# A two-layer hybrid backbone: the norm chains of layer one's latent halves staggered in separate PSUM banks, and W1 in three column passes

## The chip, the cores and the metric

The kernel runs on one core of one Trainium2 chip, as one program. The metric is the device time of one execution in microseconds. The kernel before took 2814.94 us (median of three runs, 2808.75 to 2815.92).

## The reference

Two layers work on a stream of 512 latent tokens and 256 context tokens with 1024 channels. Each layer mixes tokens (an RWKV-7 scan and gated linear attention behind one input projection, a merge projection behind them) and then applies an MLP with squared ReLU. Each of the two parts is normed and modulated before and behind it. Cut to what matters here:

```python
m_lat, m_ctx, v_new = token_mixer(h_lat, h_ctx, v_first, lp, l, rows, not last)
x_lat = x_lat + g_m * rms_norm(m_lat, norm_mix_post[l])
f_lat = sq_relu_mlp(modulate(x_lat, norm_ffn_pre[l], sh_f, sc_f), mlp_w1[l], mlp_w2[l])
x_lat = x_lat + g_f * rms_norm(f_lat, norm_ffn_post[l])
if not last:
    x_ctx = x_ctx + cg_m * rms_norm(m_ctx, norm_mix_post[l])
    f_ctx = sq_relu_mlp(modulate(x_ctx, norm_ffn_pre[l], csh_f, csc_f), mlp_w1[l], mlp_w2[l])
    x_ctx = x_ctx + cg_f * rms_norm(f_ctx, norm_ffn_post[l])
```

`rms_norm` divides by the root of the mean square over a token's 1024 channels; `modulate` norms, scales and shifts. The context counts in layer one only; its output is not needed behind the last layer.

## The kernel before

Activations lie channel by channel: 8 tiles of 128 channels by 768 columns, of which 0 to 255 are the context ("c") and 256 to 767 the latents ("l"). For the norms the latents are cut in two halves of 256 columns, "l" and "l2". An fp32 product is made of three fp32r products: a weight tile of 128 x 1024 is loaded in two halves of 256 KB (`wr`, `load_w`), each split into `wh` by ACT and `wl` by POOL or DVE, and multiplied with the split activations `sh` and `sl`. So a weight tile is 24 matmuls for each pass over columns; the result stays in a PSUM bank `d`.

`out_mlp` is the part of a layer behind the mixer: the branches' output projection (`wout`), the merge projection (`wmrg`), then four blocks of W1 (8 tiles) and W2 (8 tiles). In layer one most tiles go over the 512 latent and the 256 context columns at once. Two places are woven instead: the merge with the beginning of W1's first block, and the last block of W2 with the first tiles (12, 13, 14) of the next layer's input projection (`first_tiles`). There the tiles go column pass by column pass, so that the norm chain of some columns can run beside the matmuls of others.

A norm chain is `post_mod`: the squares of the 8 tiles are summed (`sum_sq`: ACT writes `q` or `S`, POOL adds them, small matmuls with a column of ones sum over channels), DVE and POOL form the reciprocal root `rn`, two PE transposes spread it over the partitions into a PSUM bank, DVE multiplies (`u`) and DVE and POOL in turn add to the residual `x`. Then the same again on `x`, and ACT and DVE write the next `sh` and `sl`. Both the sum and the spread statistic of a chain use one bank tile from the pool that `CB` names for it: `D0` and `D1` are pools of one PSUM bank each. A bank's tiles are handed out in the order in which the code asks for them.

`weave` sets the order of the code: the steps are the tiles of the passes; each chain is a generator of five parts, and `at` says before which step each part is asked for (offsets -1, 1, 2, 5, 6 from the chain's own step). In layer one the first entry of `halves` holds two chains, l and l2, which are stepped together.

The code's order is not yet the order of execution. `Order` collects all instructions of a segment (`flush` ends one), gives each a price and a due time by its place in the code (dense matmuls are due later by a fixed amount), and places them engine by engine as inputs, banks and buffers come free by its prices. What it decides is then fixed for each engine's queue. PE, ACT, DVE, POOL and SP (the DMA queue) each work strictly in that order. Consecutive PE calls of one `kind` are placed as one node. A segment starts from the clocks at which the one before it ended.

Of the kernel before, what the change touches and what calls it, by code (L numbers as in the profile page):

```python
# [11 lines left out]
F32 = mybir.dt.float32  # L12
# [7 lines left out]
P = 128  # L20
D = 1024
KT = 8
NCTX = 256
NLAT = 512
NT = NCTX + NLAT
NCH = NT // 64
L0 = NCTX
# [71 lines left out]

SB = 6  # L100
ACCUM = (False, True)

CFG = {
    "nfill": ((2, 2, 0, 2, 2, 1, 1, 2, 0, 2, 2, 0, 2, 1, 1, 0, 0, 0, 0), (2, 3, 0, 2, 2, 1, 2, 2, 0, 2, 2, 0, 1, 0, 0, 1, 0, 0, 0)),
# [47 lines left out]
class Order:  # L152
# [57 lines left out]
    def add(self, key, op, fn, a, k):  # L210
        out = k["out"] if "out" in k else a[0]
        ins = [x for x in (*a[(0 if "out" in k else 1):], *(v for n, v in k.items() if n != "out")) if isinstance(x, bass.AP)]
        w, n = self.width, {}
# [5 lines left out]
        if key == "PE":  # L219
            lhs = k["lhsT"] if "lhsT" in k else a[1]  # L220
# [49 lines left out]
                else:  # L270
                    n["d"] = 150.0 + 1.05 * c + (60.0 if op == "scalar_tensor_tensor" and isinstance(k.get("scalar"), bass.AP) else 0.0)
        if key == "PE":
            n["kind"] = (n["cfg"], str(lhs.dtype), op, n["w"][0][0].cap_key if n["w"] else None)
            n["calls"] = 1
            n["fill"] = n["dense"] and bool(n["w"]) and str(n["w"][0][0].cap_key).startswith("d1")
            n["side"] = bool(n["w"]) and n["w"][0][0].name.startswith("da_")
            p = self.nodes[-1] if self.nodes else None
            if GROUP and p is not None and p.get("kind") == n["kind"] and p["calls"] < (3 if lhs.dtype == F32R else 8 if n["dense"] else 16):
                p["call"].append((fn, a, k))
                p["calls"] += 1  # L280
                p["d"] += n["d"]
                p["flow"] += n["flow"]
                for x in ("w", "r"):
                    p[x] += [y for y in n[x] if y not in p[x]]
                return
# [289 lines left out]
def hybrid_kernel(ctx: ExitStack, tc: tile.TileContext, A: dict, out: bass.AP):  # L575
# [74 lines left out]
    def mm(o, a, b, start=True, stop=True):  # L650
        pe.matmul(o, lhsT=a, rhs=b, start=start, stop=stop)
# [3 lines left out]
    class Ring:  # L655
        n = 0
# [13 lines left out]
            return dps.tile(shape, dt, name=name, tag=self.tag, bufs=1)  # L670

    D0, D1 = One("d0"), One("d1")
    CB = ({"l": D0, "l2": D0, "c": D1}, {"l": D0, "l2": D1})

    def load_w(src, slots=None, lo_eng=(pool, pool), qs=(0, 1), c=None):
        halves = []
# [205 lines left out]
    def weave(dd, dw, chains, offs, then=()):  # L882
        steps = [f for g in dd for f in g] + [f for g in dw for f in g]
        nt = len(dd[0])
        at = {}
        for gi, ch in enumerate(chains):
            lim = nt * len(dd) + len(dw[0]) * gi if dw else 999
            for off in offs:
                at.setdefault(min(nt * (gi + 1) + off, lim), []).append(ch)
        for p in range(max(len(steps), max(at) + 1)):  # L890
            for chs in at.get(p, ()):
                for ch in chs:
                    next(ch, None)
            if p < len(steps):
                steps[p]()
            for at_p, f in then:
                if p == at_p:
                    f()
# [12 lines left out]

    def first_tiles(l, acts, pss, s):
        tiles = [(pss[0], None, "", 12), (pss[1], mps, "d", 13), (pss[2], ips, "i", 14)]
        tiles = [t for t in tiles if l == 0 or s == "l" or t[3] != 14]
        n = NLAT if s == "l" else NCTX
        o = L0 if s == "l" else 0
        for q in range(2):
            for ps, pl, tag, m in tiles:
                if q == 0:
                    pl = pl or (D0 if s == "l" else D1)  # L920
                    ps[s] = pl.tile([P, 512], F32, name="d", tag=tag)[:, 0:n]
                (hi, lo), = load_w(A["win"][l, m], None, (dve, pool), (q,))
                for k in range(4):
                    ah, al = acts[k + 4 * q]
                    for wi, (wt, at) in enumerate(((hi, ah), (hi, al), (lo, ah))):
                        mm(ps[s], wt[:, k, :], at[:, o:o + n], start=(q == 0 and k == 0 and wi == 0),
                           stop=(q == 1 and k == 3 and wi == 2))

    def mixer(l, acts, adas, pre, early):
# [879 lines left out]
    def out_mlp(l, last, ya, wo):  # L1809
        full = l == 0  # L1810
        st = STREAMS if full else STREAMS[:1]
        groups = STREAMS if full else GROUPS[:2]
        halves = [GROUPS[:2], GROUPS[2:]] if full else [[g] for g in GROUPS[:2]]
        nf = 3 if full else 5
        o0 = 0 if full else L0
        n0 = NT - o0
        eng = lambda j: (pool, dve)[j % 2]
# [1 line left out]
        with ExitStack() as mx:  # L1819
# [21 lines left out]
                for m in ms_:  # L1841
                    evac(m, dense(load_w(srcs[m], None, PD), acts, st), st)

            def passes(srcs, acts, evac, ms_):
                def one(m, g):
                    evac(m, dense(load_w(srcs[m], None, PD), acts(), [g]), [g])

                return [[(lambda m=m, g=g: one(m, g)) for m in ms_] for g in groups]

            late, pre = {}, [{}, {}, {}]  # L1850

# [31 lines left out]
            for c in range(4):  # L1883
                hid = {}

                def ev_h(m, ps, sts):
                    if m not in hid:
                        hid[m] = alloc_hl(("bh", "bl"), bp)
                    o, n = min(x[1] for x in sts), sum(x[2] for x in sts)
                    t = tp.tile([P, n], F32, name="t", tag="t", bufs=3)  # L1890
                    for s, o1, n1 in sts:
                        act.activation(out=t[:, o1 - o:o1 - o + n1], in_=ps[s], func=AF.Relu)
                        dve.tensor_tensor(out=t[:, o1 - o:o1 - o + n1], in0=t[:, o1 - o:o1 - o + n1], in1=ps[s], op=ALU.mult)
                    hi, lo = hid[m]
                    act.activation(out=hi[:, o:o + n], in_=t, func=AF.Copy)
                    pool.tensor_tensor(out=lo[:, o:o + n], in0=t, in1=hi.bitcast(F32)[:, o:o + n], op=ALU.subtract)

                def ev_o(m, ps, sts):
                    for s, o, n in sts:
                        if c == 0:  # L1900
                            act.activation(out=ac[m][:, o:o + n], in_=ps[s], func=AF.Copy)
                        else:
                            dve.tensor_tensor(out=ac[m][:, o:o + n], in0=ac[m][:, o:o + n], in1=ps[s], op=ALU.add)

                w1 = [A["w1"][l, 8 * c + m] for m in range(8)]
                if c == 0:
                    weave(passes(wm, lambda: mh, ev_mrg, range(8)), passes(w1, new_h, ev_h, range(nf)),
                          [[post_mod(tp, ms, l, 1, g, xs, None, l, 2, new_h) for g in gs] for gs in halves], CFG["om"][l])
                    h = late.pop("h")
                    ac = [acc.tile([P, NT], F32, name="a", tag="a") for _ in range(8)]  # L1910
                body(w1, h, ev_h, range(nf if c == 0 else 0, 8))
                w2 = [A["w2"][l, c, m] for m in range(8)]
                hd = [hid[m] for m in range(8)]
                if c < 3:
                    body(w2, hd, ev_o, range(8))

            def store_x(j, x, o, n):
                if last:
                    sp.dma_start(out=out[:, j, o - L0:o - L0 + n], in_=x[:, o:o + n])
                else:  # L1920
                    sp.dma_start(out=xdr[0][:, j, o:o + n], in_=x[:, o:o + n])

            weave(passes(w2, lambda: hd, ev_o, range(8)), [],
                  [[post_mod(tp, ac, l, 3, g, xs, store_x, l + 1, 0, None if last else new_h) for g in gs] for gs in halves], CFG["oe"][l],
                  () if last else ((16, lambda: first_tiles(l + 1, late["h"], pre, "l")), (22, lambda: first_tiles(l + 1, late["h"], pre, "c"))))
            early = {} if last else {8: load_w(A["win"][l + 1, 8], c=0)}
            od.flush()
            return late.get("h"), pre, early
# [148 lines left out]
```

## Time and profile before

| | |
|---|---|
| three runs | 2808.75 to 2815.92 us, median 2814.94 |
| profiled execution | 2812.3 us, its span 2810.5 us |
| PE busy | 95% of the span |
| DVE, ACT, POOL busy | 58%, 46%, 42% |
| granted TensorE clock | 0.977 of full speed on average |
| DMA | 276.53 MB, mean 98 GB/s |

The page says what each engine did over the whole execution. Busy shares are averages over stages with different limits, so the stages have to be looked at one by one: the output part of layer one lies between about 860 and 1600 us of the span, the mixers on either side of it.

### The profile page before, as it was taken

Reading aid. Unit: us, or ns where it says so; the run is one execution under the profiler, and the core shown is the slowest. Engines: PE = TensorE matmul, PEld = TensorE weight load, DVE = VectorE, ACT = ScalarE, POOL = GpSimd, SP = SyncE. Lnnn points to the kernel's source line nnn. Section 1 sums busy time; section 2 is a strip of 40 time slices with the busy share of each in tenths; the row PEclk is TensorE's granted clock in tenths of the full one; section 3 lists DMA queues with packets and bytes.
Section 4 is the critical chain, followed back from the end, with each engine's and each line's share of the span. In section 5 each row is a group of like instructions: output and inputs, shape, how many; then the busy total and the mean of one; then the engine's idle time right before and its main releaser. Section 6 shows DMA issues by size and latency. Waiting matters only on the chain.

```text
span 2810.5 us, 56340 instructions
## 1 busy us (share of the span) xinstructions
PE 2662.9 (95%) x22618; PEld 2229.4 (79%) x22618; DVE 1624.6 (58%) x2996; ACT 1282.8 (46%) x2606; POOL 1179.3 (42%) x1336
## 2 busy tenths in 40 slices
PE   7999999999989999999999899999989979899998
PEld 5788878788767878888888777777777768888887
DVE  6687787886687361122223636887878687622224
ACT  5554545545553452322134545555555564533333
POOL 3653534433321642223135546554444232733335
PEclk9999999999999989999999899999999999999999
DMA  6321323232226322222223344321311126433334
GB/s 238 117 88 56 115 93 119 82 96 67 78 90 238 101 73 63 64 64 61 64 64 103 121 157 125 95 81 57 108 39 40 42 62 221 124 109 98 94 97 132
DMA packets 148437, 276.53 MB, mean 98 GB/s; under 512 B 16496, under 2 KB 25456, under 8 KB 148176
## 3 DMA queue, kind: packets, MB, share of 16 engines
q1 hardware_dynamic: 148176, 272.93, 30.7%
q8 instruction: 178, 2.92, 0.4%
q14 instruction: 83, 0.68, 0.1%
HBM read 242.85 MB, written 30.02 MB: 97 GB/s over the span
## 4 chain that ended last, share of the span: by engine, by line
PE 76%; DVE 9%; POOL 4%; ACT 4%; DMA 4%; issue 3%; SPq 0%; POOLq 0%; ACTq 0%; DVEq 0%
PE d L567 58%; PE c L567 8%; PE m L567 5%; PE i L567 4%; PE da L567 1%; POOL wl L567 1%; DVE lw L567 1%; DVE ZA L567 1%; POOL S L567 1%; POOL x L567 1%; DMA ra<-in_ada_dram 1%; DVE ZS L567 1%; ACT f L567 1%; DMA wr<-in_win_dram 1%; DVE sc L567 1%
## 5 line engine op out<-in xcount | busy, mean ns | idle before, releaser
L567 PE MATMUL d<-sh,wh 128*128 128x512 f32 (+1 forms) x3280 | 1192.0, 363 | 28.1 <-ACT f L567 10.8
L567 PE MATMUL d<-sh,wl 128*128 128x512 f32 (+1 forms) x3280 | 1138.3, 347 | 16.0 <-POOL wl L567 13.4
L567 PE MATMUL d<-sl,wh 128*128 128x512 f32 (+1 forms) x3280 | 1138.3, 347 | 3.0 <-POOL sl L567 1.7
L567 POOL TENSOR_TENSOR wl<-wr,wh 128x512 fp32r<-128x512 f32 x356 | 479.9, 1350 | 750.7 <-ACT wh L567 734.8
L567 PEld LDWEIGHTS d<-sh,wh 128*128 128x128 f32 x3280 | 629.2, 192 | 128.3 <-issue 18.1
L567 PEld LDWEIGHTS d<-sh,wl 128*128 128x128 f32 x3280 | 628.1, 191 | 99.8 <-POOL wl L567 18.7
L567 PEld LDWEIGHTS d<-sl,wh 128*128 128x128 f32 x3280 | 629.6, 192 | 69.8 <-DVE sl L567 3.8
L567 ACT ACTIVATE wh<-wr 128x512 fp32r<-128x512 f32 x580 | 362.1, 627 | 495.8 <-PE d L567 389.9
L567 DVE TENSOR_TENSOR wl<-wr,wh 128x512 fp32r<-128x512 f32 x224 | 170.9, 767 | 180.4 <-ACT wh L567 171.7
L567 DVE TENSOR_TENSOR t<-t,d 128x512 f32<-128x512 f32 (+1 forms) x101 | 58.1, 577 | 315.5 <-ACT t L567 315.5
L567 POOL TENSOR_TENSOR sl<-t,sh 128x512 fp32r<-128x512 f32 (+2 forms) x72 | 104.8, 1458 | 207.1 <-ACT sh L567 207.1
L567 DVE TENSOR_TENSOR a<-a,d 128x512 f32<-128x512 f32 (+1 forms) x80 | 44.4, 554 | 228.8 <-PE d L567 228.7
L567 ACT ACTIVATE XY<-i 128x512 f16<-128x512 f32 x192 | 108.2, 593 | 91.0 <-PE i L567 89.1
L567 ACT ACTIVATE t<-d 128x512 f32<-128x512 f32 (+1 forms) x101 | 51.4, 510 | 167.0 <-PE d L567 166.6
L567 POOL TENSOR_TENSOR LTL<-AB,LTB 64x512 f16<-64x512 f32 x48 | 61.0, 1271 | 136.3 <-DVE LTB L567 98.4
L567 POOL TENSOR_TENSOR rn<-rn,C 128x2 f32<-128x2 f32 (+2 forms) x41 | 60.2, 1468 | 119.2 <-DVE rn L567 118.5
L567 POOL TENSOR_TENSOR S<-S,q 128x256 f32<-128x256 f32 x92 | 75.7, 832 | 56.5 <-ACT q L567 53.7
L567 PEld LDWEIGHTS <-XY 64*64 64x64 f16 x1920 | 64.3, 109 | 40.5 <-issue 27.8
L567 DVE TENSOR_TENSOR Q<-i,MK 128x512 f16<-128x512 f32 x120 | 82.7, 689 | 18.3 <-PE i L567 15.5
L567 ACT ACTIVATE f<-d 128x512 f32<-128x512 f32 (+1 forms) x85 | 54.3, 647 | 82.4 <-PE d L567 65.5
L567 PE MATMUL i<-Q,XY 64*64 64x64 f16 x1920 | 80.5, 197 | 7.9 <-DVE Q L567 5.0
L567 PEld LDWEIGHTS <-LTB 128*128 128x128 f16 x1344 | 60.3, 99 | 26.9 <-issue 21.1
(258 smaller groups left out, 4193.2 us busy)
## 6 DMA issues: line engine op xcount, KB each, us to landing
wr<-in_w_dram SPq DMA_DIRECT2D x304, 256.0 KB, 2.7
wr<-in_win_dram SPq DMA_DIRECT2D x180, 256.0 KB, 2.9
wa<-in_ada_dram SPq DMA_DIRECT2D x160, 256.0 KB, 2.9
wr<-in_wmrg_dram SPq DMA_DIRECT2D x64, 256.0 KB, 3.0
ra<-in_ada_dram SPq DMA_DIRECT2D x32, 256.0 KB, 5.4
wr<-in_wout_dram SPq DMA_DIRECT2D x32, 256.0 KB, 3.2
gdr<-fg SPq DMA_DIRECT2D x20, 384.0 KB, 3.0
gdr<-fg SPq DMA_DIRECT2D x20, 256.0 KB, 2.0
```

Of the source, the lines that this page charges most:

```text
L567: ins = fn(*a, **k).ins
```

## The change

Five edits, all for layer one's output part:

- `CB`: the chain of l2 uses the bank pool D1 instead of D0; the context's chain stays on D1.
- `weave` and its callers: the three column groups l, l2 and c have a chain each instead of l and l2 being stepped together. With three chains, l's step is 8, l2's is 9 (`NB` = 1) and the context's 16.
- The first tiles of W1's first block: four (`NF`) instead of three, and over l, l2 and c with 256 columns each instead of over 512 latent and 256 context columns. Each pass loads its weight tiles anew. Four tiles instead of five are left for the plain form.
- `first_tiles`: l and l2 are separate calls, from step 15 (`F0`) and 17, which load their weights anew; before it was one call for 512 columns from step 16. Both write the same bank, l the columns 0 to 255 and l2 the others. The call for c stays at step 22.
- The planner's `kind` of a matmul also holds the tensor's name where both operands are the same tensor.

For layer two `parts` has the same two groups as `halves` had, and `nf` stays 5.

```diff
+NF = 4
+NB = 1
+F0 = 15
...
-            n["kind"] = (n["cfg"], str(lhs.dtype), op, n["w"][0][0].cap_key if n["w"] else None)
+            n["kind"] = (n["cfg"], str(lhs.dtype), op, n["w"][0][0].cap_key if n["w"] else None, lhs.tensor.name if lhs.tensor is rhs.tensor else None)
...
-    CB = ({"l": D0, "l2": D0, "c": D1}, {"l": D0, "l2": D1})
+    CB = ({"l": D0, "l2": D1, "c": D1}, {"l": D0, "l2": D1})
...
             lim = nt * len(dd) + len(dw[0]) * gi if dw else 999
+            t0 = (nt, nt + NB, 2 * nt)[gi] if len(chains) == 3 else nt * (gi + 1)
             for off in offs:
-                at.setdefault(min(nt * (gi + 1) + off, lim), []).append(ch)
+                at.setdefault(min(t0 + off, lim), []).append(ch)
...
-        tiles = [t for t in tiles if l == 0 or s == "l" or t[3] != 14]
-        n = NLAT if s == "l" else NCTX
-        o = L0 if s == "l" else 0
+        tiles = [t for t in tiles if l == 0 or s != "c" or t[3] != 14]
+        c0 = NCTX if s == "l2" else 0
+        o, n = {"l": (L0, NCTX), "l2": (L0 + NCTX, NCTX), "c": (0, NCTX)}[s]
         for q in range(2):
             for ps, pl, tag, m in tiles:
-                if q == 0:
+                sk = "c" if s == "c" else "l"
+                if q == 0 and s != "l2":
                     pl = pl or (D0 if s == "l" else D1)
-                    ps[s] = pl.tile([P, 512], F32, name="d", tag=tag)[:, 0:n]
+                    ps[sk] = pl.tile([P, 512], F32, name="d", tag=tag)[:, 0:NLAT if s == "l" else n]
...
-                        mm(ps[s], wt[:, k, :], at[:, o:o + n], start=(q == 0 and k == 0 and wi == 0),
+                        mm(ps[sk][:, c0:c0 + n], wt[:, k, :], at[:, o:o + n], start=(q == 0 and k == 0 and wi == 0),
...
-        halves = [GROUPS[:2], GROUPS[2:]] if full else [[g] for g in GROUPS[:2]]
-        nf = 3 if full else 5
+        parts = GROUPS if full else GROUPS[:2]
+        nf = NF if full else 5
...
-            def passes(srcs, acts, evac, ms_):
+            def passes(srcs, acts, evac, ms_, gs):
...
-                return [[(lambda m=m, g=g: one(m, g)) for m in ms_] for g in groups]
+                return [[(lambda m=m, g=g: one(m, g)) for m in ms_] for g in gs]
...
-                    weave(passes(wm, lambda: mh, ev_mrg, range(8)), passes(w1, new_h, ev_h, range(nf)),
-                          [[post_mod(tp, ms, l, 1, g, xs, None, l, 2, new_h) for g in gs] for gs in halves], CFG["om"][l])
+                    weave(passes(wm, lambda: mh, ev_mrg, range(8), groups), passes(w1, new_h, ev_h, range(nf), parts),
+                          [[post_mod(tp, ms, l, 1, g, xs, None, l, 2, new_h)] for g in parts], CFG["om"][l])
...
-            weave(passes(w2, lambda: hd, ev_o, range(8)), [],
-                  [[post_mod(tp, ac, l, 3, g, xs, store_x, l + 1, 0, None if last else new_h) for g in gs] for gs in halves], CFG["oe"][l],
-                  () if last else ((16, lambda: first_tiles(l + 1, late["h"], pre, "l")), (22, lambda: first_tiles(l + 1, late["h"], pre, "c"))))
+            weave(passes(w2, lambda: hd, ev_o, range(8), groups), [],
+                  [[post_mod(tp, ac, l, 3, g, xs, store_x, l + 1, 0, None if last else new_h)] for g in parts], CFG["oe"][l],
+                  () if last else ((F0, lambda: first_tiles(l + 1, late["h"], pre, "l")), (F0 + 2, lambda: first_tiles(l + 1, late["h"], pre, "l2")), (22, lambda: first_tiles(l + 1, late["h"], pre, "c"))))
```

## Rows read from the trace of the kernel before

**Rows 1.** The page: busy time, share of the span and instructions of each engine.

```profile
PE 2662.9 (95%) x22618; PEld 2229.4 (79%) x22618; DVE 1624.6 (58%) x2996; ACT 1282.8 (46%) x2606; POOL 1179.3 (42%) x1336
```

**Rows 2.** Table by stages: stretch, its length, busy us, PEclk, DMA share, GB/s.

```profile
942.00:1033.00 91.00, 78.97 (x438) 69.98 (x437) 55.54 (x109) 47.36 (x109) 57.31 (x61) 0.83 0.27 83
...
1075.00:1524.00 449.00, 449.00 (x2511) 391.63 (x2511) 88.53 (x146) 124.73 (x217) 125.00 (x90) 1.00 0.22 66
1524.00:1600.00 76.00, 64.04 (x368) 57.65 (x367) 54.68 (x111) 37.03 (x83) 47.70 (x51) 0.82 0.43 130
```

**Rows 3.** Timeline of PE, stage A: start, duration, instruction [idle before, who ended it].

```profile
948.86 0.28 PE L567 MATMUL d<-sh,wh 128*128 128x256 f32 x1
...
967.50 0.38 PE L567 MATMUL d<-sh,wl 128*128 128x256 f32 x1 [2.57 <-POOL wl L567]
...
993.74 0.66 PE L567 MATMUL d<-C,rn 128*128 128x128 f32 x2 [3.17 <-DVE u L567]
...
997.33 0.79 PE L567 MATMUL d<-sh,wh 128*128 128x512 f32 x1 [0.25 <-ACT sh L567]
...
1075.77 0.39 PE L567 MATMUL d<-sh,wh 128*128 128x512 f32 x1
```

**Rows 4.** Timeline of DVE: the second statistics in A, W2's last latent tile.

```profile
978.08 0.16 DVE L567 TENSOR_SCALAR rn<-d 128x2 f32<-128x2 f32 x1 [4.58 <-PE d L567]
...
984.69 0.16 DVE L567 TENSOR_SCALAR rn<-d 128x2 f32<-128x2 f32 x1 [2.86 <-PE d L567]
986.04 1.26 DVE L567 SCALAR_TENSOR_TENSOR u<-x,AB,d 128x256 f32<-128x256 f32 x3 [1.19 <-PE d L567]
...
1523.95 0.69 DVE L567 TENSOR_TENSOR a<-a,d 128x512 f32<-128x512 f32 x1 [4.29 <-PE d L567]
```

**Rows 5.** Timeline of PE, stage B.

```profile
1570.22 0.66 PE L567 MATMUL d<-C,rn 128*128 128x128 f32 x2 [5.73 <-DVE u L567]
...
1603.52 0.50 PE L567 MATMUL d<-sh,wh 128*128 128x512 f32 x1 [0.24 <-ACT f L567]
```

**Rows 6.** Timeline of PE in a quiet stretch: first matmuls of three runs of twelve.

```profile
1432.71 0.40 PE L567 MATMUL d<-sh,wh 128*128 128x512 f32 x1
...
1435.46 0.28 PE L567 MATMUL d<-sh,wh 128*128 128x256 f32 x1
...
1436.89 0.40 PE L567 MATMUL d<-sh,wh 128*128 128x512 f32 x1
```

**Rows 7.** Groups by shape, 950 to 1030, the chains' matmuls: busy us, mean ns | idle.

```profile
L567 PE MATMUL d<-C,S 128*128 128x1 f32 x68 | 11.4, 286 | 3.1 <-DVE u L567 2.0 <-POOL S L567 1.1
L567 PE MATMUL d<-C,rn 128*128 128x128 f32 x12 | 3.1, 354 | 3.4 <-DVE u L567 3.2
```

**Rows 8.** Groups by shape, POOL, 942 to 1033.

```profile
L567 POOL TENSOR_TENSOR wl<-wr,wh 128x512 fp32r<-128x512 f32 x15 | 20.2, 1344 | 8.1 <-ACT wh L567 8.1
L567 POOL TENSOR_TENSOR S<-S,q 128x256 f32<-128x256 f32 x24 | 18.5, 783 | 13.4 <-ACT q L567 13.1 <-POOL S L567 0.2
L567 POOL TENSOR_TENSOR x<-x,u 128x256 f32<-128x256 f32 x12 | 11.0, 923 | 2.2 <-DVE u L567 2.2
L567 POOL TENSOR_TENSOR rn<-rn,C 128x2 f32<-128x2 f32 x6 | 5.0, 842 | 5.0 <-DVE rn L567 5.0
...
L567 POOL TENSOR_TENSOR sl<-t,sh 128x256 fp32r<-128x256 f32 x1 | 0.9, 940 | 1.7 <-ACT sh L567 1.7
```

**Rows 9.** Groups by shape, DVE's weight split, 1524 to 1600 and 1075 to 1524.

```profile
L567 DVE TENSOR_TENSOR wl<-wr,wh 128x512 fp32r<-128x512 f32 x12 | 11.8, 1006 | 0.3 <-ACT wh L567 0.2
...
L567 DVE TENSOR_TENSOR wl<-wr,wh 128x512 fp32r<-128x512 f32 x56 | 38.7, 692 | 66.5 <-ACT wh L567 62.4
```

**Rows 10.** Chain of waits in stage B: start, us, what.

```profile
1529.48 3.62 DMA wr<-in_w_dram
```

**Rows 11.** Table by stages: layer two's chains beside W1, end of the second mixer.

```profile
2390.00:2470.00 80.00, 70.26 (x516) 65.99 (x515) 49.01 (x90) 47.55 (x109) 60.09 (x58) 0.96 0.43 130
2000.00:2340.00 340.00, 303.07 (x3173) 247.46 (x3173) 267.42 (x512) 190.20 (x397) 131.86 (x185) 0.97 0.17 52
```

## The prediction

> **What bounds the kernel now.** I read the page's busy line first: PE is busy for 95% of the span and no other engine for more than 58% [rows 1]. So the kernel is bound by matmuls, and a change can only win where PE stands still or runs at its lower clock. The table by stages says where that is in layer one's output part: the long middle has PE busy for 449 of 449 us at a granted clock of 1.00, while the stretch around the first norm chains (942 to 1033) has 78.97 of 91 us at 0.83, and the one at the layer's end (1524 to 1600) 64.04 of 76 us at 0.82 [rows 2]. The timeline of PE and of DVE then shows the cause. The first pass of W1 over the latents begins at 997.33 and waits for `sh`, the new h [rows 3]. The second norm statistic of the first latent half is there at 978.08, that of the second half at 984.69, and only then, at 986.04, does DVE form the first part of h, of the first half [rows 4]. The two halves go in lockstep because they share the PSUM bank of `D0`: the first half's broadcast tile may not take the bank before the second half's statistic has left it, and the second half's not before DVE has read the first's eight times. That last wait stands on PE itself: 3.17 us before the transposes at 993.74 and 5.73 us before those at 1570.22 [rows 3, 5].
>
> **How much is there to win.** Twelve matmuls of 512 columns take 1435.46 - 1432.71 = 2.75 us at the full clock, twelve of 256 columns 1436.89 - 1435.46 = 1.43 us [rows 6]. A weight tile is 24 matmuls per column pass: 5.50 us for 512 columns, 2.86 us for 256, 8.36 us for both. Stage A, from the end of the merge's latent pass (948.86) to the first matmul behind the eighth W1 tile (1075.77), lasts 126.9 us [rows 3]. Its work is 8 x 2.86 (merge, context) + 3 x 5.50 + 3 x 2.86 + 5 x 8.36 = 89.8 us, and the chains' own small matmuls, at most 11.4 + 3.1 = 14.5 us, a part of it at the lower clock [rows 7]. At least 126.9 - 89.8 - 14.5 = 22.6 us are lost. Stage B goes from 1523.95, where the last latent tile of W2 is accumulated [rows 4], to 1603.52, the first matmul of the second mixer [rows 5]: 79.6 us, with 8 x 2.86 + 3 x 5.50 + 2 x 2.86 = 45.1 us of dense work and chains alike: at least 20.0 us lost.
>
> **The change part by part.**
> *Column passes.* W1's first four tiles go over 256 columns three times; before it was three tiles, over 512 and 256. On PE a pass of 512 becomes two of 256: 2 x 1.43 - 2.75 = 0.11 us for twelve matmuls. In A these are 4 tiles x 2 halves, 0.9 us; in B three tiles, 0.7 us; together 1.5 us on the path. The Trainium skill, "TensorE: Matmul & The Clock Gate", section Back-to-back issue gap, gives 262 cycles for 256 columns and 518 for 512. By it the same edit would cost 168 x 2.5 ns = 0.4 us, an estimate from that page; the rows say more, and the sum does not need the difference.
>
> *Weights.* In A tile passes go from 3 + 3 + 5 = 11 to 4 x 3 + 4 = 16, in B from 5 to 8. Each added pass is two DMAs of 256 KB, two ACT casts, one subtraction on POOL (1344 ns [rows 8]) and one on DVE (1006 ns in such a stretch, 692 in a quiet one [rows 9]). The 16 DMAs go through SP's queue, where in B the stores of x stand too. The cover is that DMA is busy for 0.27 and 0.43 of these stretches [rows 2]. Where it fails, a load costs what one costs in B's chain of waits, 3.62 us [rows 10]; I take none, and keep one such wait for the range.
>
> *Own banks and one behind the other.* l2 moves from D0 to D1. The wait of l's second broadcast for l2's statistic goes (984.69 - 978.08 = 6.6 us [rows 4]), and PE's two waits of 3.17 and 5.73 us. With l's pass over its own 256 columns, W1 can start when l alone is done. What is late next: D1 now holds l2 and then the context, so the context's first statistic waits until DVE has read l2's last broadcast. That wait stands in PE's queue, with W1's passes behind it. The end of `c`'s chain is at least 20 us of W1 passes away in A (8 x 2.86), so I put nothing down for it; in B only 6 x 2.86 = 17 us stand there.
>
> *The other engines set the new pace.* In A, from 948.86 to the end of the twelve W1 passes, POOL has 20 wl x 1.344, 22 S x 0.783, 12 x x 0.923, 6 rn x 0.842 and 12 sl of 256 x 0.940 = 26.9 + 17.2 + 11.1 + 5.1 + 11.3 = 71.6 us [rows 8]; PE has 20 x 2.86 + at most 14.5 = 71.7. They are level, so no engine hides the other, and the end depends on how densely POOL works. The bounds: 0.63 of its time, as in this stretch now (57.31 of 91 [rows 2]), and 1.00. The nearest row lies in layer two, whose halves already go one behind the other with own banks: POOL 60.09 of 80 us, 0.75, at a PE busy for 70.26 [rows 11]. There it has less work to do than PE, here as much, so I take the middle between 0.75 and 1.00, 0.87. Then the passes end at 948.9 + 71.6/0.87 = 1031.2, four tiles over all columns follow (4 x 8.36 = 33.4), and A ends at 1064.6: 11.2 us earlier. At 0.77 it is a draw.
> In B the engine with most work is DVE: 54.68 us [rows 2] and three more wl, 3.0 us: 57.7. At the same 0.87 it is done 66.3 us after 1524, at 1590.3; behind it stand the last tiles, as now 3.5 us from the end of that stretch (1600) to 1603.52. B ends at 1593.8, 9.7 us earlier. Bounds: 0.72, as now (80.1 us, 4.1 us later), and 1.00 (57.7 us, 18.3 earlier).
>
> *The grouping key.* It gains the tensor's name where both operands of a matmul are one tensor. No matmul of the listing has that; cost nothing. Everything up to this part of layer one is then issued as before. Layer two's text is the same, but the planner enters it with other clocks and may order some of it otherwise. No row prices that; what it could move is a part of the 340 - 303.07 = 36.9 us in which PE is idle late in the second mixer [rows 11], in either direction. I take none, and 6 us for the range.
>
> **Sum.** 11.2 + 9.7 = 20.9 us; the 1.5 us of halved passes lie inside PE's slack against POOL and DVE. The profiled execution took 2812.3 us (span 2810.5): 2791.4. The median of the runs, 2814.94, is 2.6 above it: 2794.
>
> **The rivals.**
> *All of it.* The chains keep to the dependencies alone and every engine stays dense: (22.6 - 0.9) + (20.0 - 0.7) = 41 us, 2774. For it: POOL ran without a gap where it had work. Against: 71.6 us of POOL in a stage of no more.
> *The wait moves to D1.* The context's first statistic blocks PE behind l2's last reads for what D0 cost, 3.17 + 5.73 = 8.9 us of the gain: 2803. For it: the same order of bank, read and in-order queue. Against: W1 passes lie between, in A.
> *Even.* POOL at 0.77 in A (a draw) and DVE at 0.80 in B (72.1 us, 4 us earlier): about 2811. For it: layer two's 0.75.
> *Slower.* The passes of 256 columns wait for their weights. PE takes 2.86 us for a pass; POOL gives a wl in 1.344 and has S, x, rn and sl of the chains between, in order. The place is the twelve W1 passes, and it decides from POOL below 0.77. The first sign is in the rows: at 967.50 PE stood 2.57 us for a wl of POOL in just such passes [rows 3]; behind it the stretch's clock has fallen to 0.83, between the levels of 1.2 and 2.4 GHz [rows 2]. At 0.70 A ends at 948.9 + 102.3 + 33.4 = 1084.6, 8.8 us later, B at its 0.72 4.1 later: 2828. DVE's wl takes 1006 ns where POOL is at work and 692 where it is not [rows 9], so more POOL work slows DVE too. The Trainium skill, "GPSIMD Engine Reference", section Specifications, says that GpSimd shares its SBUF interfaces with VectorE and contends with its instructions of two SBUF inputs; by that rule this rival gains, and the trace agrees.
>
> **How the numbers follow.** Forecast 0.40 (its own range 2783 to 2800), all of it 0.09, D1 0.16, even 0.15, slower 0.15, layer two reordered by more than 6 us 0.05, half each way. A measurement of this kernel tells 0.3%, 8.4 us, from no change: same is 2806.5 to 2823.4. Faster takes the first three and a little of the rest, 0.67; same 0.17; slower 0.16. The range reaches from all of it, 2774, to 2820, which leaves out most of the slower case and little below.
>
> **What would show it.** Right: the first W1 pass begins some 20 us or more before 997; PE's waits for DVE `u` before the transposes are gone; A's end lies near 1065 and B's near 1582 to 1584 (both gains together); POOL's busy share in A is over 0.8. Wrong: PE waits for POOL `wl` for more than some 10 us in A, or for DVE `u` before the context's small matmuls; a granted clock still near 0.83; or stages before 900 us that differ.

## The result, and the profile after

The changed kernel takes 2844.58 us (median of four runs, 2841.19 to 2845.47), against 2811.85 us for the kernel before, run beside it: a ratio of 1.011 [1.009, 1.0131]. It is slower by some 33 us where 21 us less was forecast. The profiled execution has a span of 2843.5 us, 33.0 above the 2810.5 of before.

Page of the kernel after, the busy line, which answers to [rows 1]:

```profile
PE 2683.0 (94%) x22786; PEld 2255.6 (79%) x22786; DVE 1635.6 (58%) x3008; ACT 1291.7 (45%) x2631; POOL 1189.2 (42%) x1349
```

PE is busy for 20 us more, with 168 instructions more. First where the 33.0 us lie. I use four marks that each trace has: the last latent evacuation of the merge, the first of W2, the last latent accumulation of W2, and the first instruction of the second mixer on ACT. Timeline of ACT and DVE, kernel after (start, duration, instruction):

```profile
947.58 0.60 ACT L570 ACTIVATE a<-d 128x512 f32<-128x512 f32 x1 [2.39 <-PE d L570]
...
1086.35 0.60 ACT L570 ACTIVATE a<-d 128x512 f32<-128x512 f32 x1 [2.23 <-PE d L570]
...
1527.77 0.69 DVE L570 TENSOR_TENSOR a<-a,d 128x512 f32<-128x512 f32 x1 [4.74 <-PE d L570]
...
1615.39 1.11 ACT L570 ACTIVATE thw<-f,MU 128x512 f32<-128x512 f32 x2
```

From the first to the second mark is stage A here, from the third to the fourth stage B, behind the fourth layer two. The tables by stretch between these marks (stretch, length, busy us of PE, PEld, DVE, ACT, POOL, granted clock, DMA share, GB/s), first of before, then of after; they answer to [rows 2]:

```profile
949.06:1082.97 133.91, 121.88 (x694) 108.31 (x693) 65.94 (x126) 63.13 (x135) 73.75 (x70) 0.89 0.26 79
1523.95:1603.60 79.65, 67.45 (x393) 60.86 (x391) 54.80 (x111) 39.50 (x88) 49.54 (x53) 0.83 0.42 128
1603.60:2373.02 769.42, 715.46 (x7524) 574.34 (x7525) 570.97 (x1051) 407.67 (x852) 337.70 (x447) 0.98 0.29 91
```

```profile
947.58:1086.35 138.77, 122.64 (x786) 113.05 (x785) 74.94 (x135) 69.12 (x154) 82.47 (x80) 0.91 0.30 95
1527.77:1615.39 87.62, 71.45 (x461) 68.18 (x459) 57.16 (x114) 43.06 (x93) 53.10 (x56) 0.77 0.45 135
1615.39:2404.02 788.63, 728.36 (x7530) 584.01 (x7531) 570.18 (x1051) 407.33 (x852) 338.26 (x447) 0.96 0.28 89
```

A lasts 4.9 us longer and B 8.0 longer, both of which should have become shorter; with the smaller differences between the marks the second mixer starts 1615.39 - 1603.60 = 11.8 us later. The other 21.2 us are layer two's: 1228.1 us from the fourth mark to the end, 1206.9 before, though its text is the same. Nearly all of them lie in the second mixer (788.6 us against 769.4).

In A PE has 1 us more work, and 16.1 us of idle time for 12.0. What it waits for is in the table of waits of PE over A (engine, line, releaser: us in total, times, longest), first before, then after:

```profile
PE d L567 <- DVE u L567: 5.1, 3, 3.2
PE d L567 <- POOL wl L567: 3.9, 3, 2.6
PE d L567 <- ACT sh L567: 1.4, 2, 1.2
PE d L567 <- POOL S L567: 1.1, 1, 1.1
```

```profile
PE d L570 <- POOL wl L570: 7.3, 8, 1.5
PE d L570 <- POOL S L570: 3.2, 3, 1.7
PE d L570 <- DVE u L570: 2.0, 2, 1.1
PE d L570 <- POOL rn L570: 1.6, 3, 0.7
PE d L570 <- ACT wh L570: 0.9, 1, 0.9
```

Before there were a few long waits, for the bank above all; after there are seventeen mostly short ones in these rows, for split weights and the statistics' sums. In B PE idles for 16.2 us (12.2 before) and is busy for 4.0 us more, at 0.77 instead of 0.83. Timeline of PE, kernel after, three places that answer to [rows 5]:

```profile
1568.68 0.55 PE L570 MATMUL d<-sh,wh 128*128 128x256 f32 x1 [3.27 <-ACT sh L570]
...
1577.67 0.98 PE L570 MATMUL d<-C,S 128*128 128x1 f32 x4 [3.22 <-DVE u L570]
...
1604.33 0.69 PE L570 MATMUL d<-C,rn 128*128 128x128 f32 x2 [2.95 <-POOL rn L570]
```

The second row is the context's sum, which waits on D1 until DVE has read l2's statistic.

### The profile page after: what moved, and what is told of

The parts are those of the page before. It is cut to its first block, busy times and chain, and to the rows that moved or that the text cites. A ratio compares the mean times of both kernels' runs of the same rounds, so it can differ in the third digit from the quotient of the medians.

```text
span 2843.5 us, 56785 instructions
## 1 busy us (share of the span) xinstructions
PE 2683.0 (94%) x22786; PEld 2255.6 (79%) x22786; DVE 1635.6 (58%) x3008; ACT 1291.7 (45%) x2631; POOL 1189.2 (42%) x1349
## 5 line engine op out<-in xcount | busy, mean ns | idle before, releaser
L570 PE MATMUL d<-sh,wh 128*128 128x512 f32 (+1 forms) x3336 | 1206.1, 362 | 33.8 <-DVE y L570 15.9
L570 PE MATMUL d<-sh,wl 128*128 128x512 f32 (+1 forms) x3336 | 1152.6, 346 | 19.3 <-POOL wl L570 16.1
L570 PE MATMUL d<-sl,wh 128*128 128x512 f32 (+1 forms) x3336 | 1151.7, 345 | 3.1 <-POOL sl L570 1.7
L570 POOL TENSOR_TENSOR wl<-wr,wh 128x512 fp32r<-128x512 f32 x364 | 490.5, 1350 | 751.5 <-ACT wh L570 734.9
L570 PEld LDWEIGHTS d<-sh,wh 128*128 128x128 f32 x3336 | 645.1, 193 | 131.3 <-issue 21.4
L570 PEld LDWEIGHTS d<-sh,wl 128*128 128x128 f32 x3336 | 643.7, 193 | 101.2 <-POOL wl L570 21.4
L570 PEld LDWEIGHTS d<-sl,wh 128*128 128x128 f32 x3336 | 645.6, 194 | 65.9 <-DVE sl L570 3.3
L570 ACT ACTIVATE wh<-wr 128x512 fp32r<-128x512 f32 x596 | 371.3, 627 | 489.1 <-PE d L570 386.9
L570 DVE TENSOR_TENSOR wl<-wr,wh 128x512 fp32r<-128x512 f32 x232 | 179.5, 779 | 182.3 <-ACT wh L570 176.5
L570 POOL TENSOR_TENSOR sl<-t,sh 128x768 fp32r<-128x768 f32 (+2 forms) x77 | 104.7, 1360 | 215.9 <-ACT sh L570 206.2
L570 PEld LDWEIGHTS <-LTB 128*128 128x128 f16 x1344 | 60.6, 100 | 28.7 <-issue 22.7
```

The source lines that it names most:

```text
L570: ins = fn(*a, **k).ins
```

## Experiments

In "after, old order" and in all kernels from "A alone" to "A with shared weights" layer two's instructions are issued in the order of before on every engine, so that its re-planning is kept out; layer one is planned anew for each edit. All results (A, B and layer two from the profiled execution, us; the median of the runs, that of before in the same job, and the ratio with its 95% interval):

| kernel | A | B | layer two | median | before | ratio |
|---|---|---|---|---|---|---|
| before | 133.9 | 79.6 | 1206.9 | | | |
| after | 138.8 | 87.6 | 1228.1 | 2844.6 | 2811.9 | 1.011 [1.009, 1.0131] |
| after, old order in layer two | 138.7 | 87.7 | 1216.6 | 2834.2 | 2811.6 | 1.0077 [1.0062, 1.0092] |
| before, new order in layer two | 133.4 | 79.4 | 1224.2 | 2828.3 | 2811.6 | 1.0058 [1.0046, 1.007] |
| A alone | 139.0 | 80.3 | 1223.3 | 2833.5 | 2811.6 | 1.007 [1.0055, 1.0085] |
| B alone | 133.4 | 84.4 | 1215.7 | 2825.0 | 2811.6 | 1.0047 [1.0034, 1.0061] |
| chains alone | 133.2 | 81.9 | 1214.3 | 2824.7 | 2813.0 | 1.0037 [1.0022, 1.0052] |
| passes alone | 140.0 | 85.1 | 1216.5 | 2835.4 | 2814.1 | 1.0065 [1.005, 1.008] |
| l2 loads no weights | 130.1 | 80.6 | 1208.9 | 2814.5 | 2814.1 | 0.9998 [0.9986, 1.0011] |
| context on a third bank | 142.0 | 86.6 | 1220.3 | 2839.3 | 2814.1 | 1.0081 [1.0066, 1.0096] |
| A with shared weights | 134.6 | 78.4 | 1216.4 | 2821.5 | 2814.1 | 1.0028 [1.0015, 1.0041] |

A, B and layer two are of one execution each, and they scatter. Nine profiles have the layer one of before in them (before, before with the new order, and the seven delays at the end of this section): in these A is 131.3 to 133.9 us and B 74.9 to 79.6, and the second mixer starts at 1596.0 to 1603.6, less the delay. The row "before" stands at the upper end of each. So a difference of 2 or 3 us in A, or of 5 in B, says nothing by itself.

**After, with the old order in layer two.** A table gives each engine the sequence of the kernel before:

```diff
-            for n in cands[e]:
+            if held is None:
+                cs = cands[e]
+            else:
+                cs = [ns[held[e][0]]] if held[e] and not want[held[e][0]] else []
+            for n in cs:
```

> The changed kernel, with layer two (second mixer and second output part) issued in exactly the order that the planner gave it in the kernel before. Theory 1 (the order is the cause): layer one's output part ends 11 to 12 us later than before (stage A +4.9, stage B +8.4 in the profiles, the rest noise), and layer two takes again 1207 us from its first mixer matmul to the end, not 1228: about 12 us over the kernel before, ratio 1.004. Rival (layer two pays for what it inherits: the phase of TensorE's clock, DMAs under way, buffer slots): layer two takes 1228 us in the old order too, ratio 1.011.

10.4 us of the change's loss go (2844.6 to 2834.2), and layer two takes 11.5 us less: 1216.6, half way between the 1207 of the theory and the 1228 of the rival. 22.7 us remain, of which layer one's two places are 11.4 (the mixer starts at 1614.96).

**Before, with the new order in layer two.** The opposite: the same table with the sequences of after, on the unchanged kernel.

> The kernel before, with layer two issued in the order that the planner gave it in the changed kernel; layer one untouched. Theory 1: layer two takes 1228 us in place of 1207, about 21 us over the kernel before, ratio 1.0075. Rival (inherited state): layer two takes 1207 us, ratio 1.000.

The new order alone costs 16.8 us (1.0058), with layer one untouched. So both signs agree: the planner's other course through layer two is worse by 10 to 17 us. The second mixer's rows say how: first this kernel, then after with the old order.

```profile
1601.25:2386.50 785.25, 724.69 (x7530) 580.98 (x7531) 569.97 (x1051) 407.94 (x853) 340.95 (x447) 0.96 0.28 89
```

```profile
1614.96:2392.92 777.96, 724.03 (x7524) 581.85 (x7525) 571.45 (x1051) 407.81 (x852) 337.26 (x446) 0.96 0.28 90
```

The new order leaves PE idle for 785.25 - 724.69 = 60.6 us (60.3 in the kernel after), the old one for 53.9, as before (54.0). But the old order, behind the changed layer one, has PE busy for 724 us instead of 715 with the same matmuls: they ran longer at the lower clock (0.96 for 0.98).

**A alone, B alone, the chains alone.** The pieces of the change, taken apart:

```diff
-    CB = ({"l": D0, "l2": D1, "c": D1}, ...)
+    CB = ...    # stage A: l2 on D1 or on D0
+    CE = ...    # stage B: l2 on D1 or on D0
...
-   [[post_mod(...)] for g in parts]
+   [[post_mod(...) for g in gs] for gs in pairs]    # lockstep, where not staggered
```

> Only the first place is changed (l2's chain on D1 and one step behind l's, W1's first four tiles in three passes); the layer's end (W2, first tiles, their chains) as before; layer two held to the order of before. Theory 1: the stage from the last latent merge tile to the eighth W1 tile takes about 132 us as in the changed kernel (126.9 before), the layer's end 79 to 80 us as before, total about +5 us, ratio 1.002. If the two places lean on each other, the sum of this run's and of the next one's excess is not that of the first run.

> Only the layer's end is changed (l2's chain on D1 and one step behind, first tiles of the next layer in three passes); the merge and W1 as before; layer two held to the order of before. Theory 1: the layer's end takes about 88 us (79.6 before), stage A 126.9 us, total about +8 us, ratio 1.003.

> Both places: only the chains are changed (l2's chain on D1 and one step behind l's); W1's three first tiles go over 512 and 256 columns as before, the next layer's first tiles too; layer two held to the order of before. If the three column passes cost the time (more weights to load and split for the same matmuls), stage A and the layer's end take no more than before (126.9 and 79.6 us between the same marks) or some us less. If the staggering itself costs it, stage A takes 131 us and the end 87 us as in the changed kernel.

A alone has the whole 139.0. B alone has 84.4, 4.8 of the 8.0 us: in B the places do not simply add up, and the second mixer starts 6.6 and 1.6 us later than before, 8.2 of the 11.4 us of both together. Both kernels took longer than expected (1.007 and 1.0047 for 1.002 and 1.003), as layer two took 1223.3 and 1215.7 us in its old order. The chains alone (staggered, own banks, the column passes of before) have an A like that of before, 133.2, and a B 2.3 us above it, which no unchanged profile reaches. PE's waits over A in that kernel:

```profile
PE d L586 <- POOL rn L586: 7.7, 4, 6.0
PE d L586 <- POOL S L586: 5.1, 3, 3.0
PE d L586 <- ACT sh L586: 1.8, 1, 1.8
```

The waits for DVE's `u` on the bank are gone, as forecast, and 12.8 us for POOL's root and sums of squares stand in their place (1.1 for the sums before). I read this so: the sum, the root, the residual and the next sum follow one another, and the bank had only been the last to be ready.

**The passes alone, and the passes without their weights.**

```diff
-                    evac(m, dense(load_w(srcs[m], None, PD), acts(), [g]), [g])
+                    w = kept["w"] if g[0] == "l2" and full else load_w(srcs[m], None, PD)
+                    kept["w"] = w
+                    evac(m, dense(w, acts(), [g]), [g])
...
```

> Only the three column passes of the change, in both places (four W1 tiles, first tiles of l and l2 apart, weights loaded anew for each pass); the chains of l and l2 go in lockstep on D0 as before; layer two is issued in the order of before. Theory (the added passes with their weights cost, the chains gain next to nothing): stage A (last latent merge evacuation to first W2 evacuation) 137 to 140 us as with the chains staggered (139.0), against 133 to 134 without the passes; stage B 82 to 86; time about 1.004 to 1.008 of before. Rival (it is the combination of staggered chains, D1 and passes that costs): A and B within 1 us of before (133.9, 79.6), time within 0.3%.

> After, with layer two in the order of before; l2's four W1 passes and l2's first tiles load and split no weights of their own but multiply with weights that l's pass has left in its buffers (so those columns get other products in the W1 passes: that part of the computation is changed, all matmuls remain). It takes away 14 DMAs, 14 ACT casts and 14 subtractions, ten of the 20 wl beyond the merge's in A among them being no more than eight. Theory (the weights' refill through the two buffers makes the passes dear): A falls from 138.7 to 131 to 135 us, B from 87.7 by 2 to 5 us, time 8 to 12 us below the same kernel with its loads (2834). Rival 1 (the passes are dear for the 256-column matmuls themselves and PE's lower clock, not for weights): A 137 to 139, B 86 to 88, time as 2834 within 4 us. Rival 2 (the staggered chains could after all give what was forecast once POOL is free of the extra wl): A 124 to 129.

l2's passes take the weights of l's last tile, in the first tiles of layer two as well as in W1. The two runs say where layer one's loss comes from. The passes alone, without staggering and on the old bank, cost the whole of A (140.0) and 5.5 us of B. With every matmul of the change left in place and only l2's loads and splits taken away, A falls by 8.6 us and B by 7.1, and the median is that of before. That is 19.7 us below the kernel with its loads, where 8 to 12 were expected, as layer two falls too, to 1208.9. The two stretches without l2's loads, beside those of after above:

```profile
947.56:1077.69 130.13, 117.96 (x786) 109.77 (x785) 68.37 (x131) 64.65 (x146) 76.43 (x76) 0.93 0.27 86
1519.11:1599.71 80.60, 65.71 (x461) 63.12 (x459) 54.05 (x111) 39.72 (x88) 47.44 (x53) 0.83 0.42 127
```

The counts of PE are equal (786, 461). In A half of the gain is less waiting (12.2 for 16.1 us of idle time), half a busy time 4.7 us shorter at 0.93 instead of 0.91. In B it is nearly all busy time: 65.71 for 71.45, at 0.83 for 0.77. POOL's busy time falls by 6.0 us in A and 5.7 in B, on an engine that had 56 and 35 us to spare there. So the weights do not cost as a sum of work on one engine. That they cost by when they come, and that the clock rises because they go, is my reading: no run changes their time alone. The rival by which the chains would pay once POOL is free (A 124 to 129) is missed by 1.1 us only, less than A's scatter; against the nine unchanged profiles A is 1.2 to 3.8 us shorter and B 1.0 to 5.7 longer, and the second mixer's start, 1599.71, lies among theirs. Even without the second load layer one gains nothing.

**The context on a third bank.**

```diff
-    CB = ({"l": D0, "l2": D1, "c": D1}, {"l": D0, "l2": D1})
+    CB = ({"l": D0, "l2": D1, "c": D2}, {"l": D0, "l2": D1})    # D2: cps
```

> After, with layer two in the order of before; the context's chain takes its two bank tiles from the cps pool of the dense tiles' ring instead of D1, so it never waits for l2's reads. Theory (the D1 wait is one of several waits in line and worth at most what PE waited there): PE's wait of 3.2 us before the context's small matmuls in B goes, B falls from 87.7 by 1 to 3 us, A by 0 to 1 us, time 1 to 4 us below 2834. Rival (the D1 wait is what B lost, as the prediction's rival had it): B falls by 5 us or more, to 82 or less.

B is 1.1 us shorter, A 3.3 longer, and the time does not fall, where 1 to 4 us were expected. PE's waits over B:

```profile
PE d L586 <- POOL rn L586: 5.5, 4, 2.5
PE d L586 <- DVE wl L586: 4.8, 2, 4.5
PE d L586 <- ACT f L586: 1.3, 1, 1.3
```

The wait for DVE's `u` (4.1 us after) is gone, and one of 4.5 us for a split weight takes its place. The D1 wait was there, but it was one in a line of waits; the 5 us or more of the rival do not come.

**A with shared weights.** A version with all products right and no second load: two tiles over l, the same two over l2 from the same buffers, then the next two.

```diff
-    passes(w1, new_h, ev_h, range(nf), parts)
+    [[f(m, g) for m0 in range(0, n, 2) for g in (0, 1) for m in (m0, m0 + 1)], [f(m, 2) for m in range(n)]]
```

> Stage A alone: chains of l and l2 one behind the other with own banks and W1's first four tiles in column passes, but in the order l0 l1, l2 of 0 and 1, l2 l3, l2 of 2 and 3, then the context's four, so that l2 takes the split weights that l has left in the two buffers and loads none; stage B as before, layer two in the order of before. Theory (weights): A 130 to 134 us against 139.0 with the weights loaded anew, and the time at or below that of before, 2800 to 2815. Rival (the passes and the chains cost without the weights too, by PE's clock or by the chains' order on DVE and POOL): A 136 to 140, time 2822 to 2835.

A is 134.6 against 139.0 with the loads, which agrees with the weights as cause, though the order of the passes changed too; it lies between the theory's range and the rival's, and is no gain on the 131.3 to 133.9 of before. The mixer starts at 1600.95, within the scatter of before. The time misses what I expected: 2821.5, with a layer two of 1216.4 us. It does not beat the kernel before.

**Delays of the unchanged kernel.** That left layer two's other part: 1214 to 1223 us in the old order behind most edits, 1206.9 behind the old layer one. Seven kernels repeat the first matmuls of some tiles in the dense middle of layer one, and change nothing else:

```diff
+                    calls = [(calls[0][0], calls[0][1], dict(calls[0][2], stop=True))] * 3 + calls
```

> The kernel before, every instruction in its order; in the quiet middle of layer one's output part nine matmuls are issued again (six of 512 columns, three of 256; a result that is overwritten), 1.7 us of PE and nothing else. Why did layer two take 1216.6 us in its old order (first run) and not 1207? Theory A (where in time layer two starts decides how often the clock falls in it): layer two takes longer here too, 5 to 15 us, with the granted clock down in the mixer's last third. Theory B (what layer two inherits, such as other buffers and other waits, decides): layer two takes 1207 us, the total is 1.7 us above the kernel before.

> The same with fifteen repeated matmuls of 512 columns, 3.4 us of PE. Theory A: another layer-two time than 1207 us by up to 15 us; if the effect comes round again with the start, this one and the one of 1.7 us differ from each other. Theory B: 1207 us, 3.4 us above the kernel before in total.

> The same with 48 repeated matmuls of 512 columns and three of 256, 11.3 us of PE: layer two begins as late as in the changed kernel. Theory A: layer two takes about 1216 us as in the run that held the old order, total about 20 us above the kernel before. Theory B: 1207 us, total 11 us above.

> The kernel before, with 24 added matmuls of 512 columns (first matmuls of tiles issued four times) in the dense middle of layer one: a pure PE delay of 24 x 0.229 = 5.5 us, orders unchanged. Theory growth (layer two loses 0.7 us per us of later start): layer two +4, median +9 to +10 against before. Rival step (layer two has two courses, about 1207 and about 1216, and the start's small shifts decide between them): layer two in the profile either within 3 us of 1207 or between 1213 and 1222, median +5.5 or +14.5 or between, if executions are mixed.

> The same with 36 matmuls, a delay of 8.25 us. Growth: layer two +6, median +14. Step: layer two near 1207 or 1216, median +8 to +17, no larger extra than behind 5.5 us.

> The same with 75 matmuls, a delay of 17.2 us. Growth: layer two +12, median +29. Step: layer two near 1207 or 1216 to 1222, median +17 to +27.

> The same with 99 matmuls, a delay of 22.7 us. Growth: layer two +16, median +39. Step: layer two near 1207 or 1216 to 1222, median +23 to +33.

| delay | layer two, profiled | median, over before | beyond the delay | ratio |
|---|---|---|---|---|
| 1.7 | 1206.6 | 3.6 | 1.9 | 1.0011 [0.9995, 1.0026] |
| 3.4 | 1215.8 | 4.4 | 1.0 | 1.0014 [1.0001, 1.0028] |
| 5.5 | 1213.3 | 7.1 | 1.6 | 1.0025 [1.0014, 1.0036] |
| 8.25 | 1210.4 | 13.6 | 5.4 | 1.0048 [1.0036, 1.0061] |
| 11.3 | 1220.6 | 19.7 | 8.4 | 1.0055 [1.0036, 1.0074] |
| 17.2 | 1215.0 | 21.9 | 4.7 | 1.0084 [1.0066, 1.0103] |
| 22.7 | 1216.6 | 26.9 | 4.2 | 1.0096 [1.0081, 1.0111] |

By the medians the kernel takes 1 to 8 us more than the delay when layer two merely starts later, so a part of the loss may be nothing that the change does there. The intervals set this extra clear of zero behind 8.25 and 17.2 us, and just so behind 22.7; behind 11.3 us the ratio gives 4.2 us of extra and the median 8.4. It does not grow with the delay: 22.7 us bring 4.2, where growth at the rate of the 8.4 us behind 11.3 (0.7 per us) would have brought 16. Nor is it a clean step between two values; the profiled ones run from 1206.6 to 1220.6. Those are single executions, and sixteen of the unchanged kernel in one job run from 2805.45 to 2820.62 us, a span as wide. What goes with it is the clock. The second mixer behind delays of 8.25 and 22.7 us, one fence each:

```profile
1604.20:2378.01 773.81, 718.51 (x7524) 576.24 (x7525) 567.79 (x1051) 407.14 (x853) 337.03 (x446) 0.98 0.29 91
```

```profile
1622.37:2397.21 774.84, 722.97 (x7524) 581.62 (x7525) 569.79 (x1051) 407.31 (x853) 337.42 (x446) 0.96 0.29 91
```

One place, 550 to 575 us into layer two, before and after with the old order (same sequence on each engine; 5950 and 5952 matmuls lie ahead of it):

```profile
2153.60:2178.60 25.00, 22.32 (x281) 18.76 (x280) 19.99 (x39) 17.81 (x40) 12.98 (x18) 1.00 0.12 34
```

```profile
2164.96:2189.96 25.00, 23.08 (x217) 19.52 (x217) 17.80 (x34) 15.21 (x34) 11.78 (x18) 0.76 0.11 33
```

The same code does 281 matmuls in 25 us at 1.00 in one and 217 at 0.76, about half of the time at 1.2 GHz, in the other. What tips such a place to the lower level is open. The start alone does not show it: one at 1600.95 gave 1216.4 us, one at 1601.49, in another kernel, 1206.6.

## Why the prediction was wrong

*What bounds, and how much could be won.* The stages and their losses were read rightly, but a loss is not a gain. Of A's 22.6 us the bank's waits were 5.1 on PE, and with the bank's waits gone those for the chain's own sums and roots came to 12.8. This is the first step that failed: with all of the change in place but l2's loads A gained 1.2 to 3.8 us, not 11.2, and B nothing of its 9.7.

*The first sign.* W1 was to begin some 20 us or more before 997. Timelines of DVE, ACT and PE, kernel after:

```profile
975.05 0.15 DVE L570 TENSOR_SCALAR rn<-d 128x2 f32<-128x2 f32 x1
...
980.17 1.26 DVE L570 SCALAR_TENSOR_TENSOR u<-x,AB,d 128x256 f32<-128x256 f32 x3 [2.46 <-PE d L570]
983.33 1.53 DVE L570 SCALAR_TENSOR_TENSOR sl<-u,MT,sh 128x256 fp32r<-128x256 f32 x3 [1.89 <-ACT sh L570]
```

```profile
982.79 1.29 ACT L570 ACTIVATE sh<-u,MT 128x256 fp32r<-128x256 f32 x3
...
994.27 0.38 ACT L570 ACTIVATE a<-d 128x256 f32<-128x256 f32 x1 [2.70 <-PE d L570]
```

```profile
985.24 0.28 PE L570 MATMUL d<-sh,wh 128*128 128x256 f32 x1
...
988.21 0.39 PE L570 MATMUL d<-sh,wl 128*128 128x256 f32 x1 [1.52 <-POOL wl L570]
...
991.27 0.39 PE L570 MATMUL d<-sh,wl 128*128 128x256 f32 x1 [0.85 <-POOL wl L570]
...
997.25 0.39 PE L570 MATMUL d<-sh,wh 128*128 128x256 f32 x1 [0.86 <-ACT wh L570]
...
998.60 0.38 PE L570 MATMUL d<-sh,wl 128*128 128x256 f32 x1 [0.85 <-POOL wl L570]
...
1079.15 0.39 PE L570 MATMUL d<-sh,wh 128*128 128x512 f32 x1
```

l's second statistic comes 3.0 us earlier than in [rows 4] and the first part of h 5.9 us earlier. The merge's last context tile is evacuated at 994.27. Up to there PE has issued 222 matmuls of 256 columns from 947.38 on, and the merge's eight context passes are only 192 of them: 30 are W1's. The first, at 985.24, is the one whose weight loads wait for ACT and then for DVE, behind the first `sh` and `sl` of h. So W1 does begin early, 12.1 us before the 997.33 of [rows 3], beside the merge's last tile. But its eight tiles end at 1079.15, 3.4 us later than the 1075.77 of before: part of the early start is spent on waits for `wh` and `wl`, four of which stand above.

*Weights: "I take none".* This step failed next. I looked for their cover in the DMA, and that held: PE waited for no transfer, and the DMA share rose only from 0.26 to 0.30 in A. ACT's casts did wait 4.6 us in A for a transfer, and not before, but without l2's loads they waited 4.4 as well. The refill goes through two buffers of `wh` and `wl`, though, and through ACT, POOL and DVE, where it stands in order among the chain's instructions. It measured 8.6 us in A and 7.1 in B, where a reserve of one wait of 3.62 us was kept for the range [rows 10].

*The pace of 0.87.* In A I forecast the end of the twelve passes at 1031.2; the first matmul over 512 columns is issued at 1044.25, after POOL had been busy for 65.82 of 96.85 us:

```profile
947.40:1044.25 96.85, 80.72 (x546) 76.14 (x545) 64.89 (x119) 54.00 (x127) 65.82 (x68) 0.88 0.32 103
```

That is 0.68, below the 0.77 at which the step called it a draw; the work was 65.82 us of the 71.6 forecast, and A ended at 1079.15 instead of 1064.6. The level of POOL's and PE's work was no reason for density; POOL's sum of work was not the limit. Groups of POOL in 942 to 1033, kernel after (busy us, mean ns | idle before, releasers):

```profile
L570 POOL TENSOR_TENSOR wl<-wr,wh 128x512 fp32r<-128x512 f32 x17 | 23.7, 1400 | 5.0 <-ACT wh L570 4.9
L570 POOL TENSOR_TENSOR S<-S,q 128x256 f32<-128x256 f32 x23 | 18.7, 820 | 11.2 <-ACT q L570 8.4 <-PE d L570 2.6
...
L570 POOL TENSOR_TENSOR sl<-t,sh 128x256 fp32r<-128x256 f32 x6 | 4.6, 760 | 9.2 <-ACT sh L570 9.2
```

While PE waited for POOL, POOL waited for ACT, and ACT for PE, as 2.70 us before the evacuation at 994.27. I read this as a ring of in-order queues in which nobody is full; no run cuts the ring in one place. An engine's sum of work bounds such a stage from below only. In B DVE was busy for 57.16 us as forecast (57.7), but of 87.62, 0.65, under the lower bound of 0.72.

*The rivals.* "Slower" was right in kind, with A 4.9 and B 8.0 later for its 8.8 and 4.1; its sign, over 10 us of waits for POOL's `wl`, came to 7.3. Its other ground was read too strongly: the row of DVE's `wl` at 692 ns [rows 9] is of a stretch in which POOL was busy for 125 of 449 us [rows 2], not idle, and from 942 to 1033 the same subtraction took 990 ns before and 1033 after. "The wait moves to D1" was there too, 3.2 us in B, but worth 1.1 us at most. "All of it" and the forecast fell.

*Layer two: "I take none, and 6 us for the range".* It took 21.2 us more, nearly two thirds of the loss: 11.5 by the other order (10.4 in the median, and 16.8 with the new order on the old layer one), 9.7 with the old order at the later start, where the delays gave 1 to 8. The planner enters layer two with other clocks and came to another order; that the one of before was a lucky draw is not shown by two orders. What the 9.7 us hang on stays open: single executions of the unchanged kernel differ by 15 us.

*What held.* Everything up to layer one's merge is issued in the same order, as forecast, no matmul in the trace of before has one tile as both operands, which is what the grouping key asks for, and PE's busy time in A grew by only 0.8 us (0.9 forecast for the halved passes). The last agreement is partly luck: the clock in A differed too, 0.91 for 0.89.

## What to carry to other kernels

Splitting a column pass to start earlier doubles the traffic of weights for those columns through every engine that prepares them: look at the buffers and the in-order queues of that preparation, not only at the transfers, or let both halves use one load. An earlier start is not an earlier end: ask what will feed the consumer from there on. Where a planner orders the work, hold the order of the untouched part while you judge an edit; otherwise a new draw of it, worth 10 to 17 us here, is booked on the edit. And before reading a few us of one stage in one profile, see how far the same stage scatters where nothing was changed.

## What the runs showed of the hardware

The time at the lower clock differs between executions of the same instructions. With one order of layer two and different starts, it took between 1206.6 and 1220.6 us in the profiles, and its second mixer had PE busy for 715 to 727 us with the same matmuls. A later start is not needed for this: sixteen executions of the unchanged kernel in one job took from 2805.45 us, at a mean granted clock of 0.979, to 2820.62, at 0.974. In stage B, with layer one unchanged, the same 393 matmuls kept PE busy for 63.68 us at 0.86 behind the delay of 8.25 us and for 68.07 at 0.82 behind that of 5.5. With the change PE idled there for 14.9 us without and 16.2 us with l2's loads, and its busy time differed by 5.7 us, at 0.83 and 0.77. What sets the level each time is open.
